# First feed-forward product of a two-layer trunk: four of seven half products joint in 512 columns, one weight sum loaded anew, weight splits handed out one unit later

## The chip, the cores and the metric

One core of one Trainium2 chip. The metric is the device time of one execution in microseconds, lower is better. The engines meant below are PE (TensorE, matrix products), DVE (VectorE), ACT (ScalarE), POOL (GpSimd) and SP (SyncE, which here only issues DMAs). PE writes its sums to PSUM; everything else lies in SBUF.

## The reference

A sequence of 512 positions with 1024 features passes two layers. Each has an attention part and then a dense part with 4096 hidden features; the change touches the dense part alone:

```
y = rmsnorm(x, g_ff)
x = x + (square(relu(y @ W1))) @ W2      # W1: 1024 x 4096, W2: 4096 x 1024, float32
```

The kernel keeps nearly float32 accuracy with PE's faster fp32r type: a value is split into a rounded part (hi) and the rest (lo), and a product is three matmuls, hi by hi, hi by lo and lo by hi, summed in PSUM.

## The kernel before

**Two products, each in seven parts.** The hidden features are handled in four groups (`g`) per layer. In a group both products, `h @ W1` and then `F @ W2`, are done with seven block products instead of eight (Strassen's scheme in Winograd's form): sums and differences of quarter blocks are made first, seven half-size products follow, and the results are added up. The first product has the halves "1" to "7" (`HALVES`, L50), each for `c` = 0 and 1, so 14 units per group; the kernel calls these units q. A q unit is 24 matmuls of 128 weights by 256 moving columns: eight weight blocks, and for each the three products of `three` (L295 to L300). The second product has seven forms ("11", "21", "x1" and so on) of two f units each, with 48 matmuls of 512 columns per form.

**Weights.** `_Weights` holds one list of units. A unit's raw weights come by DMA as 512 KB. `split_part` makes the pair: ACT copies raw to fp32r, `whi` (L131), DVE subtracts to get `wlo` (L132). The feed-forward part has five such pairs. `next` (called when a unit's matmuls are written) calls `do_split`, which writes the split of the unit four ahead and then what hangs on that unit in `then`: a weight sum (`sum1`, L859, on DVE in L862), a load (`fetch`, L869, and `fill`, L850, on SP), or a load that the DMA adds to what is in SBUF (issued by POOL in L852, L864, L876). The sum for half "7" is made in that last way in `sum1` (L864): the raw block of half "1" stays in its buffer and POOL adds another block to it.

**Moving operands.** `h_hi` and `h_lo` are the split of the normalised x; `T_hi` and `T_lo` that of its differences, which `opening(0)` to `opening(3)` make (L884: one DVE operation, then ACT for hi and DVE for lo in L245) during the first group of a layer. `MOVES` says which half reads which 256 columns of h or T.

**Taps.** When a unit's matmuls are written, `tap` (L960) writes what empties its PSUM bank: ACT copies (L970, L975, L977), DVE adds (L972, L978, L983). `bend` queues relu and square on ACT (L967) in `put_off`, and `come_to` writes the queued work behind the next unit's split. The results are F[0] to F[3]; for F[3] (half "4") relu reads PSUM directly. `behind_3` makes the differences of F for the second product (F4 in L1001, F0 in L1003, F1 in L996), and `roll` splits F[1] and F[3] into `Ah` and `Al`, the moving operand of forms "11" and "21" (forms "x1" to "x4" read splits of the other F, `Ahx` and `Alx`). `gather` adds the sums of the forms into Y (L1025).

**Order.** ACT and DVE run in the order in which the program writes their work: `line` chains them. An instruction whose input is not there holds up all behind it on its engine. PE's order is the program's too, with a few matmuls pulled ahead by the scheduler. The loads are `paced` by the last split.

Of the kernel before, what the change touches and what calls it, by code (L numbers as in the profile page):

```python
# [17 lines left out]
P = 128  # L18
# [31 lines left out]
HALVES = ("1", "2", "5", "6", "7", "3", "4")  # L50
LAYS = (("5", 1), ("6", 0), ("6", 1), ("7", 0))
# [46 lines left out]
class _Weights:  # L98
    def __init__(self, nc, dram, rawp, splp):
        self.nc, self.dram, self.rawp = nc, dram, rawp  # L100
        self.loaded = self.split = self.used = self.turn = 0
        self.raw, self.tiles, self.home, self.then, self.lows, self.came = {}, {}, {}, {}, {}, {}
# [44 lines left out]
    def do_split(self, n, ahead=None):  # L147
        while self.split < min(n, self.stop):
            i = self.split
            kind = _UNITS[i][0]  # L150
            if ahead is not None and i > ahead and self.owner.get(self.spot(i), -1) >= ahead:
                break
            if kind not in "fq":
                self.load(_SLOT[i] + 1)
            self.split_part(i, 0, 1024)
# [21 lines left out]
def trunk(ctx, tc, xT, w, w1, w2, gains, gfin, lamv, cos, sin, out):  # L177
# [8 lines left out]
    banks = {"t": 2, "mm": 2, "s": 3, "o": 1}  # L186
    turn = [0]

    def bank(tag, name):
        if tag == "any":  # L190
            tag = ("mm", "s", "s", "mm", "s")[turn[0] % 5]
            turn[0] += 1
        return ps.tile([P, 512], F32, tag=tag, name=name, bufs=banks[tag])
# [6 lines left out]
    h_hi = cp.tile([P, KC, S], F32R, tag="h_hi", name="h_hi")  # L200
    h_lo = cp.tile([P, KC, S], F32R, tag="h_lo", name="h_lo")
# [132 lines left out]
    for l in range(L):  # L334
        last = l == L - 1
        with ExitStack() as actx:
# [496 lines left out]
            T_hi = fr.tile([P, KC, S], F32R, tag="T_hi", name=f"T_hi{l}")  # L833
            T_lo = fr.tile([P, KC, S], F32R, tag="T_lo", name=f"T_lo{l}")
# [11 lines left out]
            def fill(what, g, c):  # L846
                t = homes[(what, c)] if what in "yw" else kept["x.z".index(what)][c]
                for q in {"y": "1", "z": "2", "x": "5", "w": "4"}[what] + {"y": "7", "x": "63"}.get(what, ""):
                    W.raw[_AT[("q", l, g, q, c)]] = t
                paced(nc.sync.dma_start(t, quad1(g, {"y": "11", "z": "12", "x": "21", "w": "22"}[what], c)))  # L850
                if what == "x":
                    nc.gpsimd.dma_start(t, quad1(g, "22", c), accum_op=ALU.add)  # L852
# [6 lines left out]
            def sum1(what, g, c):  # L859
                i = _AT[("q", l, g, "5", c)]  # L860
                t, by = W.raw[i], W.raw[_AT[("q", l, g, "1" if what == "y" else "2", c)]]
                line(v=nc.vector.tensor_add(t, t, by))  # L862
                if what == "y":
                    nc.gpsimd.dma_start(by, quad1(g, "21", c), accum_op=ALU.add)  # L864
# [14 lines left out]
            def then(kind, g, form, c, fn, *args):  # L879
                W.then.setdefault(_AT[(kind, l, g, form, c)], []).append(lambda: fn(*args))  # L880

# [24 lines left out]
            for g in range(GROUPS):  # L906
                for c in range(GP // 2):
                    then("q", g, "5", c, sum1, "y", g, c)
                    then("q", g, "6" if g else "7", c, sum1, "z", g, c)
                    then("q", g, "2" if g else "7", c, fetch, g, "21", c)  # L910
# [23 lines left out]
        with ExitStack() as fctx:  # L934
# [7 lines left out]
            for c in range(GP // 2):  # L942
                fill("w", 0, c)
            W.free = False
            MOVES = {"1": (0, hi_t, 0), "2": (4, hi_t, 0), "3": (4, lo_t, 0), "4": (4, hi_t, 1), "5": (0, hi_t, 1),
                     "6": (4, lo_t, 1), "7": (0, lo_t, 1)}

            def mover(q, cc):
                k, t, which = MOVES[q]
                a, b = ((h_hi, h_lo), (T_hi, T_lo))[which]  # L950
                return a[:, k + cc, t], b[:, k + cc, t]
# [8 lines left out]
            def tap(q, c, pt):  # L960
                def f(n):
                    return F[n][:, 512 * c : 512 * c + 512]

                def bend(n, scale=1.0, src=None):
                    for o, i, fn, by in ((f(n), src, AF.Relu, scale), (f(n), None, AF.Square, 1.0)):
                        put_off.append(lambda o=o, i=i, fn=fn, by=by: line(
                            nc.scalar.activation(o, o if i is None else i, fn, scale=by)))  # L967

                if q == "1":
                    line(nc.scalar.copy(f(1), pt))  # L970
                elif q == "2":
                    line(v=nc.vector.tensor_add(f(1), f(1), pt))  # L972
                    bend(1)
                elif q == "6":
                    line(nc.scalar.copy(f(0), pt))  # L975
                elif q == "7":
                    line(nc.scalar.copy(f(2), pt))  # L977
                    line(v=nc.vector.tensor_add(f(2), f(2), sums[("b", c)]))  # L978
                    bend(2, -1.0)
                elif q == "4":  # L980
                    bend(3, -1.0, pt)
                elif q == "3":
                    line(v=nc.vector.tensor_add(f(0), f(0), pt))  # L983
                    bend(0)
# [3 lines left out]
            def roll(form):  # L988
                nm = f"{form}{l}"
                hi = rolls.tile([P, 1024], F32R, tag="Ah", name="Ah" + nm)  # L990
                lo = rolls.tile([P, 1024], F32R, tag="Al", name="Al" + nm)
                rolled[form] = hi, lo
                return split(hi, lo, F[FSLOT[form]])
# [13 lines left out]
            def behind_4(late=False):  # L1007
                line(*roll("21"))
                if late:
                    less(1, 4, 1)  # L1010
                less(3, 1, 3)
# [18 lines left out]
            def turned(tb, j):  # L1030
                pt = bank("t", f"xT{tb}{j}")
# [19 lines left out]
            def back(c):  # L1051
                pt = bank("t", f"yT{l}{c}")
# [54 lines left out]
            for g in range(GROUPS):  # L1107
                end = g == GROUPS - 1
                kinds = iter(("s", "s", "s", "mm", "mm", "o"))
                for q in HALVES:  # L1110
                    for c in range(GP // 2):
                        n = {("2", 0): 1, ("5", 0): 2, ("3", 0): 3}.get((q, c))
# [4 lines left out]
                        spot = {"1": "a", "2": "c", "5": "b", "3": "b"}.get(q, "a")  # L1117
                        if q in "125":
                            sums[(spot, c)] = bank(next(kinds), f"f{q}{l}{g}{c}")
                        pt = sums[(spot, c)]  # L1120
                        for i in range(2):
                            for cc in range(4):
                                ops = three(pt[:, 256 * i : 256 * i + 256], wpair(u, 4 * i + cc), mover(q, cc),
                                            q in "125" and i == cc == 0, i == 1 and cc == 3, q not in "125")
                                if i == cc == 0 and (q, c) != ("1", 0):
                                    behind(ops[0], pe_end)
                        pe_end = ops[2]
                        tap(q, c, pt)
                        if (g, q, c) == (1, "1", 0):
                            ptr = bank("t", f"rs_m{l}")  # L1130
# [14 lines left out]
                        if g == 0 and (q, c) == ("4", 0):  # L1145
                            put_off.append(lambda: behind_3(1))
                        if c:
                            put_off.append({
                                "27"[g == 0]: lambda: line(*roll("11")),
                                "3": lambda: behind_3(0 if g == 0 else None),  # L1150
                                "4": lambda: behind_4(g == 0),
                            }.get(q, lambda: None))
                come_to()
                chains = {}
                for f, form in enumerate(FORMS):
                    chain, i, j = TAPS[form]
                    fresh_bank = chain not in chains
                    if fresh_bank:
                        chains[chain] = [bank(("s", "s", "s", "mm", "mm", "o")[2 * len(chains) + r], f"{form}{l}{g}{r}")
                                         for r in range(2)]  # L1160
# [4 lines left out]
                    for r in range(2):  # L1165
# [38 lines left out]
                        if end and not last:  # L1204
# [4 lines left out]
                            if form == "x4":  # L1209
                                for c_ in CAME[2 * r : 2 * r + 2]:  # L1210
                                    back(c_)
# [104 lines left out]
```

## Time and profile before

| | us |
|---|---|
| median of three runs | 1120.8 (1119.42 to 1121.47) |
| the profiled execution | 1119.62 |
| its span in the profile | 1117.8 |
| PE busy | 1109.3 |
| DVE busy | 929.5 |
| ACT busy | 709.5 |
| the q units of group 0, layer 0 | 239.96 to 280.27 |
| the q units of group 2, layer 0 | 398.33 to 438.64 |

The span leaves out 1.82 us that lie around it in the profiled execution. Times inside it are given in us from the span's start. The page of the profile lists busy time by engine, then groups of equal instructions; the timeline lists single instructions with the idle time ahead of each and what ended it; a view of windows sums a stretch by engine. A matmul's duration there includes its passage through the array and overlaps the next one, so PE's rate is read from the distance of starts.

### The profile page before, as it was taken

What the parts mean: (1) busy time and instruction counts of PE and PEld (TensorE: products, weight loads), DVE (VectorE), ACT (ScalarE), POOL (GpSimd) and SP (SyncE); (2) the same over time, 40 slices, a digit from 0 to 9 for tenths busy, and PEclk for the clock granted to TensorE, in tenths of its full rate; (3) what the DMA queues carried; (4) which work ended last, traced back from release to release, by engine and by line L of the source; (5) the groups of instructions that cost most, each with busy time, mean ns of one, the idle gap of its engine ahead of it and who ended that gap; (6) DMA issues with size and microseconds to landing.
All of it is one profiled execution on the core that took longest, in us unless ns stands there. A gap on an engine that the chain in (4) does not pass through costs nothing.

```text
span 1117.8 us, 17696 instructions
## 1 busy us (share of the span) xinstructions
PE 1109.3 (99%) x6654; PEld 985.1 (88%) x6654; DVE 929.5 (83%) x1230; ACT 709.5 (63%) x1113; POOL 176.9 (16%) x257
## 2 busy tenths in 40 slices
PE   9999999999999999999999999999999999999997
PEld 7888989889889899899888889888998998998986
DVE  7878789788897877878888787897988888888787
ACT  6546666677767557567555467675777665565675
POOL 1001334210210110201000014440101102011022
PEclk9999999999999999999999999999999999999999
DMA  7746334266887776876537463523578768859665
GB/s 249 208 123 203 114 116 114 81 170 188 186 197 214 167 176 204 189 190 158 123 113 208 119 177 113 157 77 142 105 229 185 189 189 187 206 138 202 172 135 148
DMA packets 60613, 183.37 MB, mean 164 GB/s; under 512 B 7536, under 2 KB 8816, under 8 KB 60528
## 3 DMA queue, kind: packets, MB, share of 16 engines
q1 hardware_dynamic: 46416, 131.62, 37.1%
q0 software_dynamic: 13824, 50.34, 25.7%
q8 instruction: 53, 0.87, 0.3%
q10 hardware_dynamic: 288, 0.28, 0.1%
q14 instruction: 32, 0.26, 0.1%
HBM read 154.95 MB, written 2.10 MB: 140 GB/s over the span
## 4 chain that ended last, share of the span: by engine, by line
PE 85%; DVE 5%; DMA 4%; issue 3%; ACT 2%; POOL 1%; POOLq 0%; DVEq 0%; SPq 0%; ACTq 0%
PE f L300 8%; PE f L298 8%; PE f L299 8%; DMA q<-in_w 3%; PE x L299 2%; PE x L298 2%; PE x L300 2%; PE wo L298 2%; PE wo L299 2%; PE wo L300 2%; DVE wlo L132 1%; DMA st1d1q<-hl1d1k 1%; PE T1s L623 1%; PE T0s L623 1%; PE v0u L298 1%
## 5 line engine op out<-in xcount | busy, mean ns | idle before, releaser
L132 DVE TENSOR_TENSOR wlo<-q,whi 128x1024 fp32r<-128x1024 f32 x184 | 223.6, 1220 | 23.9 <-ACT whi L131 22.6
L131 ACT ACTIVATE whi<-q 128x1024 fp32r<-128x1024 f32 x184 | 191.2, 1052 | 65.3 <-DMA q<-in_w 32.3
L298 PE MATMUL f<-T_hi,whi 128*128 128x256 f32 x512 | 145.5, 284 | 0.0
L300 PE MATMUL f<-T_hi,wlo 128*128 128x256 f32 x512 | 144.9, 283 | 0.0
L299 PE MATMUL f<-T_lo,whi 128*128 128x256 f32 x512 | 144.9, 283 | 0.0
L876 POOL DMA_DIRECT2D q<-in_w x64 | 56.2, 913 | 366.2 <-DVE wlo L132 346.4
L298 PE MATMUL f<-h_hi,whi 128*128 128x256 f32 x384 | 108.8, 283 | 0.0
L299 PE MATMUL f<-h_lo,whi 128*128 128x256 f32 x384 | 108.7, 283 | 0.0
L300 PE MATMUL f<-h_hi,wlo 128*128 128x256 f32 x384 | 108.7, 283 | 0.0
L299 PEld LDWEIGHTS f<-T_lo,whi 128*128 128x128 f32 x512 | 98.3, 192 | 0.0
L298 PEld LDWEIGHTS f<-T_hi,whi 128*128 128x128 f32 x512 | 98.3, 192 | 0.0
L300 PEld LDWEIGHTS f<-T_hi,wlo 128*128 128x128 f32 x512 | 98.2, 192 | 0.0
L967 ACT ACTIVATE F<-F 128x512 f32<-128x512 f32 x112 | 70.4, 629 | 21.7 <-DVE F L972 17.8
L131 ACT ACTIVATE whi<-raw 128x1024 fp32r<-128x1024 f32 (+1 forms) x58 | 55.7, 970 | 31.7 <-PE wo L299 6.9
L298 PEld LDWEIGHTS f<-h_hi,whi 128*128 128x128 f32 x384 | 73.7, 192 | 0.4
L299 PEld LDWEIGHTS f<-h_lo,whi 128*128 128x128 f32 x384 | 73.7, 192 | 0.3
L300 PEld LDWEIGHTS f<-h_hi,wlo 128*128 128x128 f32 x384 | 73.7, 192 | 0.1
L132 DVE TENSOR_TENSOR wlo<-raw,whi 128x1024 fp32r<-128x1024 f32 (+1 forms) x58 | 68.1, 1186 | 5.7 <-ACT whi L131 5.7
L245 ACT ACTIVATE Ahx<-F 128x1024 fp32r<-128x1024 f32 x32 | 34.0, 1061 | 52.1 <-PE x L299 24.4
L245 DVE TENSOR_TENSOR Alx<-F,Ahx 128x1024 fp32r<-128x1024 f32 x32 | 39.2, 1225 | 8.6 <-ACT Ahx L245 8.6
L245 DVE TENSOR_TENSOR Al<-F,Ah 128x1024 fp32r<-128x1024 f32 x24 | 29.4, 1224 | 18.0 <-ACT Ah L245 18.0
L556 POOL TENSOR_TENSOR sig1s<-sig1s,C1s 128x128 f32<-128x128 f32 (+3 forms) x32 | 28.5, 892 | 57.6 <-DVE C1s L553 46.7
(994 smaller groups left out, 3242.0 us busy)
## 6 DMA issues: line engine op xcount, KB each, us to landing
q<-in_w SPq DMA_DIRECT2D x100, 512.0 KB, 5.1
q<-in_w POOLq DMA_DIRECT2D x84, 512.0 KB, 7.0
raw<-in_w SPq DMA_DIRECT2D x62, 512.0 KB, 4.2
yw<-in_w SPq DMA_DIRECT2D x12, 512.0 KB, 4.5
yw<-in_w POOLq DMA_DIRECT2D x12, 512.0 KB, 5.6
cs<-in_w SPq DMA_DIRECT2D x8, 512.0 KB, 7.9
ww<-in_w SPq DMA_DIRECT2D x8, 512.0 KB, 4.0
x<-in_xT SPq DMA_DIRECT2D x8, 256.0 KB, 4.2
```

The costliest lines, as they stand in the source:

```text
L131: h = nc.scalar.activation(hi[:, a:b], raw[:, a:b], AF.Copy)
L132: self.last = h, nc.vector.tensor_tensor(out=lo[:, a:b], in0=raw[:, a:b], in1=hi[:, a:b].bitcast(F32), op=ALU.subtract)
L245: return nc.scalar.activation(hi, src, AF.Copy), nc.vector.tensor_tensor(out=lo, in0=src, in1=hi.bitcast(F32), op=ALU.subtract)
L298: return (nc.tensor.matmul(pt, ah, bh, start=first, stop=False, skip_group_check=onto), nc.tensor.matmul(pt, ah, bl, start=False, stop=Fal ...
L299: nc.tensor.matmul(pt, ah, bl, start=False, stop=False, skip_group_check=onto),
L300: nc.tensor.matmul(pt, al, bh, start=False, stop=last, skip_group_check=onto))
L556: nc.gpsimd.tensor_mul(sig[:, 0:wd], sig[:, 0:wd], C[:, 1 : wd + 1])
L623: nc.tensor.transpose(pt[:, n * P : (n + 1) * P], u["w"][qi][:, kb * P : (kb + 1) * P], ident)
L876: paced(nc.gpsimd.dma_start(t, quad(g, q, c), accum_op=ALU.add))
L967: nc.scalar.activation(o, o if i is None else i, fn, scale=by)))
```

## The change

- **Order of halves**: "1", "2", "6", "5", "3", "7", "4" in place of "1", "2", "5", "6", "7", "3", "4".
- **Joint halves**: for "1", "2", "6" and "4", `whi` by hi and `whi` by lo become one matmul of 512 columns (two runs of 256, h_hi and h_lo now being halves of one tile, as T_hi and T_lo are). It leaves hi and lo sums side by side in a full bank, two banks per unit in place of one. `wlo` by hi stays a matmul of 256 columns. A unit is then 16 matmuls and not 24; "5", "3" and "7" stay as they were.
- **Taps**: the two sides have to be added when they are read. "1" is copied by ACT from PSUM to PSUM (two of 512); "2", "7" and "4" read in pieces of 256, by ACT and by DVE; "6" goes to F[0] and to a bank `fb` in four ACT copies of 256; "3" and "5" accumulate on `fb`. For F[3] the order is now ACT copies, DVE adds, ACT relu and square. F[3] is rolled in two halves of 512, the first behind unit 4 c0.
- **Weights**: half "7" loads its first block again (SP) and POOL adds the other, rather than building on the buffer of half "1": 16 more loads of 512 KB. The sum for "6" is written just ahead of its split (`first`).
- **Splits**: `W.next("q", 1)` hands out a split one unit later, three ahead of the one whose matmuls are written.

In all ACT gets 120 more instructions, DVE 72, SP 16 more loads, and PE 1024 matmuls of 256 columns become 512 of 512.

```diff
-HALVES = ("1", "2", "5", "6", "7", "3", "4")
+HALVES = ("1", "2", "6", "5", "3", "7", "4")
...
-                for q in {"y": "1", "z": "2", "x": "5", "w": "4"}[what] + {"y": "7", "x": "63"}.get(what, ""):
+                if what == "7":
+                    t = homes["y", c] if g else (F[3], kept[1][0])[c]
...
-                if what == "x":
-                    nc.gpsimd.dma_start(t, quad1(g, "22", c), accum_op=ALU.add)
+                if what in "x7":
+                    nc.gpsimd.dma_start(t, quad1(g, "22" if what == "x" else "21", c), accum_op=ALU.add)
...
-                if what == "y":
-                    nc.gpsimd.dma_start(by, quad1(g, "21", c), accum_op=ALU.add)
...
+                def take(n, kind, lows):
+                    for h, t in zip(halves, sums[kind, c]):
+                        line(nc.scalar.copy(F[n][:, h], t[:, 256:512] if lows else t[:, 0:256]))
+
+                def more(n, kind, lows):
+                    for h, t in zip(halves, sums[kind, c]):
+                        line(v=nc.vector.tensor_add(F[n][:, h], F[n][:, h], t[:, 256:512] if lows else t[:, 0:256]))
...
                 elif q == "4":
-                    bend(3, -1.0, pt)
+                    take(3, "a", True)
+                    more(3, "a", False)
+                    bend(3, -1.0)
...
-                        u = W.next("q")
+                        u = W.next("q", 1)
...
+                                if joint:
+                                    steps[0].append((both_of(to), a[0], moved[2]))
+                                    steps[1].append((to[:, 0:256], a[1], moved[0]))
...
-                        if g == 0 and (q, c) == ("4", 0):
-                            put_off.append(lambda: behind_3(1))
+                        if (q, c) == ("4", 0):
+                            put_off.append(lambda: line(*roll("21", 0, 512)))
+                            if g == 0:
+                                put_off.append(lambda: behind_3(1))
```

**DVE where the q units of group 2, layer 0, end and form "21" begins.** The names: `F30` is F[3], `F40`, `F00`, `F10` the results that `behind_3` makes, `wlo104` and `wlo105` the two units of form "21", `Al210` the lo part of the rolled F[3]; the numbers behind an underscore only tell tiles apart. Before, from the last add into F[0] to the first gathering into Y:

```order
L983 TENSOR_TENSOR F00_2566<-F00_2566,f5021_4436 128x512
L132 TENSOR_TENSOR wlo104_4650<-q10_0_2560,whi104_4649 128x1024
L1001 TENSOR_TENSOR F40_2757<-F20_2568,F00_2566 128x1024
L1003 TENSOR_TENSOR F00_2566<-F10_2567,F00_2566 128x1024
L996 SCALAR_TENSOR_TENSOR F10_2567<-F40_2757,F10_2567 128x1024
L132 TENSOR_TENSOR wlo105_4684<-q11_0_2561,whi105_4683 128x1024
L245 TENSOR_TENSOR Al210_4717<-F30_2569,Ah210_4716 128x1024
L996 SCALAR_TENSOR_TENSOR F30_2569<-F10_2567,F30_2569 128x1024
L1025 TENSOR_TENSOR Y0_2756<-Y0_2756,11020_4721 128x512
L1025 TENSOR_TENSOR Y0_2756<-Y0_2756,11021_4722 128x512
L245 TENSOR_TENSOR Alx10_4764<-F40_2757,Ahx10_4763 128x1024
```

Of the change, from the row behind F4 (`F40`) on:

```order
L1043 TENSOR_TENSOR F00_2564<-F10_2565,F00_2564 128x1024
L1036 SCALAR_TENSOR_TENSOR F10_2565<-F40_2755,F10_2565 128x1024
L997 TENSOR_TENSOR F30_2567<-F30_2567,fa0200_4197 128x256
L997 TENSOR_TENSOR F30_2567<-F30_2567,fa0201_4198 128x256
L132 TENSOR_TENSOR wlo104_4583<-q10_0_2559,whi104_4582 128x1024
L254 TENSOR_TENSOR Al210_4590<-F30_2567,Ah210_4589 128x512
L997 TENSOR_TENSOR F30_2567<-F30_2567,fa0210_4199 128x256
L997 TENSOR_TENSOR F30_2567<-F30_2567,fa0211_4200 128x256
L254 TENSOR_TENSOR Al210_4590<-F30_2567,Ah210_4589 128x512
L1036 SCALAR_TENSOR_TENSOR F30_2567<-F10_2565,F30_2567 128x1024
L1065 TENSOR_TENSOR Y0_2754<-Y0_2754,11020_4618 128x512
L132 TENSOR_TENSOR wlo105_4646<-q11_0_2560,whi105_4645 128x1024
```

The split of `wlo105` has moved from the place behind `F10`, ahead of the roll, to a place behind four adds, both halves of the roll and a row of Y. On ACT `whi105` moved alike: it stood ahead of relu and square of F[3], and now stands behind them and both rolled halves:

```order
L993 COPY F30_2567<-fa0200_4197 128x256
L993 COPY F30_2567<-fa0201_4198 128x256
L131 ACTIVATE whi104_4582<-q10_0_2559 128x1024
L989 ACTIVATE F30_2567<-F30_2567 128x512 x2
L254 ACTIVATE Ah210_4589<-F30_2567 128x512
L993 COPY F30_2567<-fa0210_4199 128x256
L993 COPY F30_2567<-fa0211_4200 128x256
L989 ACTIVATE F30_2567<-F30_2567 128x512 x2
L254 ACTIVATE Ah210_4589<-F30_2567 128x512
L131 ACTIVATE whi105_4645<-q11_0_2560 128x1024
L254 ACTIVATE Ahx10_4665<-F40_2755 128x1024
```

Each `x2` is a relu and a square. ACT's copies from `fa` come first, and between them and these two DVE must have added.

**PE at the start of form "21", group 2, layer 0.** The rows with the waits that they carry. Before, from the first matmul of the form:

```order
L298 MATMUL 21020_4749<-whi104_4649,Ah210_4716 128x512 [waits PE_49,Activation_49]
L299 MATMUL 21020_4749<-wlo104_4650,Ah210_4716 128x512 [waits DVE_49]
L300 MATMUL 21020_4749<-whi104_4649,Al210_4717 128x512 [waits DVE_49]
L298 MATMUL 21020_4749<-whi104_4649,Ah210_4716 128x512
L299 MATMUL 21020_4749<-wlo104_4650,Ah210_4716 128x512
L300 MATMUL 21020_4749<-whi104_4649,Al210_4717 128x512
L298 MATMUL 21020_4749<-whi105_4683,Ah210_4716 128x512
L299 MATMUL 21020_4749<-wlo105_4684,Ah210_4716 128x512
```

Of the change, from the seventh:

```order
L307 MATMUL 21021_4652<-whi104_4582,Ah210_4589 128x512 [waits PE_49]
L307 MATMUL 21020_4651<-whi105_4645,Ah210_4589 128x512 [waits Activation_49]
L308 MATMUL 21021_4652<-wlo104_4583,Ah210_4589 128x512
L309 MATMUL 21021_4652<-whi104_4582,Al210_4590 128x512
L307 MATMUL 21021_4652<-whi104_4582,Ah210_4589 128x512
L308 MATMUL 21021_4652<-wlo104_4583,Ah210_4589 128x512
L309 MATMUL 21021_4652<-whi104_4582,Al210_4590 128x512
L307 MATMUL 21021_4652<-whi105_4645,Ah210_4589 128x512
L307 MATMUL x1020_4695<-whi106_4669,Ahx10_4665 128x512 [waits PE_49,Activation_49]
L307 MATMUL x1021_4696<-whi106_4669,Ahx10_4665 128x512 [waits PE_49]
L308 MATMUL 21020_4651<-wlo105_4646,Ah210_4589 128x512 [waits DVE_49]
```

Of the first product of the form, the second unit's weights (`whi105`) are wanted by the seventh matmul before and by the eighth in the change. What follows in the change is mixed with matmuls of form "x1", whose operands `Ahx10` and `whi106` ACT makes behind `whi105`.

**ACT and PE in the first group of layer 0.** ACT in the change from the tap of unit 1 c0 (the bank `fa` copied to the bank `fc`) on; `T0` is T_hi by `opening(1)`, `whi36` the weights of unit 6 c0:

```order
L1002 COPY fc0000_2783<-fa0000_2763 128x512
L1002 COPY fc0001_2784<-fa0001_2764 128x512
L254 ACTIVATE T0_2563<-hx0mdl_2569 128x4x256
L131 ACTIVATE whi36_2791<-q10_0_2559 128x1024
L1002 COPY fc0010_2811<-fa0010_2765 128x512
L1002 COPY fc0011_2812<-fa0011_2766 128x512
L131 ACTIVATE whi37_2816<-q11_0_2560 128x1024
L993 COPY F10_2565<-fc0000_2783 128x256
```

PE before, where unit 2 c0 ends (`f2000`) and 2 c1 begins (`f2001`):

```order
L298 MATMUL f2000_2834<-h_hi_73,whi34_2673 128x256
L299 MATMUL f2000_2834<-h_lo_74,whi34_2673 128x256
L300 MATMUL f2000_2834<-h_hi_73,wlo34_2674 128x256
L298 MATMUL f2001_2866<-h_hi_73,whi35_2711 128x256
L299 MATMUL f2001_2866<-h_lo_74,whi35_2711 128x256
```

PE in the change at the same place (`fc0001` and `fc0010`):

```order
L1174 MATMUL fc0001_2784<-h_73,wlo34_2672 128x256
L1174 MATMUL fc0001_2784<-h_73,whi34_2671 128x512
L1174 MATMUL fc0001_2784<-h_73,wlo34_2672 128x256
L1174 MATMUL fa0001_2764<-T0_2563,whi36_2791 128x512 [waits Activation_49]
L1174 MATMUL fc0010_2811<-h_73,whi35_2709 128x512 [waits Activation_49]
L1174 MATMUL fc0010_2811<-h_73,wlo35_2710 128x256
```

A matmul of unit 6 c0 stands ahead of unit 2 c1 here and waits for `whi36`, and the first of 2 c1 waits for the copy that ACT makes behind it. Before, 2 c1 followed 2 c0 with nothing of a later unit between them.

More of the change, by code (lines that the diff above doesn't have):

```diff
@@ L154, in do_split @@
                 self.load(_SLOT[i] + 1)
+            self.first.pop(i, lambda: None)()
             self.split_part(i, 0, 1024)
@@ L184, in trunk, with one, some @@
     ps = ctx.enter_context(tc.tile_pool(name="ps", bufs=2, space=PSUM))
-    banks = {"t": 2, "mm": 2, "s": 3, "o": 1}
+    banks = {"t": (0, 1), "mm": (2, 3), "s": (4, 5, 6), "o": (7,)}
+    calls = dict.fromkeys(banks, 0)
+    def one(k, name):
+        return ps.tile([P, 512], F32, tag=f"k{k}", name=name, bufs=1)
+    def some(ks, name):
+        return [one(k, f"{name}{n}") for n, k in enumerate(ks)]
     turn = [0]
@@ L949, in mover @@
                 k, t, which = MOVES[q]
-                a, b = ((h_hi, h_lo), (T_hi, T_lo))[which]
-                return a[:, k + cc, t], b[:, k + cc, t]
+                m = (h2, T2)[which]
+                return m[:, 0, k + cc, t], m[:, 1, k + cc, t], m[:, :, k + cc, t]
             sums, put_off = {}, []
@@ L969, in tap @@
                 if q == "1":
-                    line(nc.scalar.copy(f(1), pt))
+                    sums["c", c] = some((4 + 2 * c, 5 + 2 * c), f"fc{l}{g}{c}")
+                    for to, t in zip(sums["c", c], sums["a", c]):
+                        line(nc.scalar.copy(to, t))
                 elif q == "2":
-                    line(v=nc.vector.tensor_add(f(1), f(1), pt))
-                    bend(1)
-                elif q == "6":
-                    line(nc.scalar.copy(f(0), pt))
+                    take(1, "c", False)
@@ new lines, in tap @@
+                    more(1, "c", True)
+                elif q == "6":
+                    take(0, "a", False)
+                    sums["b", c] = one(4 + c, f"fb{l}{g}{c}")
+                    for i, t in enumerate(sums["a", c]):
+                        line(nc.scalar.copy(sums["b", c][:, 256 * i : 256 * i + 256], t[:, 256:512]))
+                    bend(1)
+                elif q == "5":
+                    line(nc.scalar.copy(F[2][:, at : at + 512], sums["b", c]))
+                elif q == "3":
+                    o = F[0][:, at : at + 512]
+                    line(v=nc.vector.tensor_add(o, o, sums["b", c]))
+                    bend(0)
@@ L986, in trunk, with roll @@
+                    bend(3, -1.0)
             rolled = {}
[L988 to L993, printed above, removed]
+            def roll(form, a=0, b=1024):
+                if a == 0:
+                    nm = f"{form}{l}"
+                    rolled[form] = [rolls.tile([P, 1024], F32R, tag=t, name=t + nm) for t in ("Ah", "Al")]
+                hi, lo = rolled[form]
+                return split(hi[:, a:b], lo[:, a:b], F[FSLOT[form]][:, a:b])
@@ L1030, in turned @@
             def turned(tb, j):
-                pt = bank("t", f"xT{tb}{j}")
+                pt = one(6 + (tb + j) % 2, f"xT{tb}{j}")
                 for k in range(4):
@@ L1116, in trunk @@
                         come_to()
[L1117 to L1120, printed above, removed]
+                        spot = {"2": "c", "5": "b", "3": "b"}.get(q, "a")
+                        if (q, c) == ("1", 0):
+                            for c_ in range(GP // 2):
+                                sums["a", c_] = some((2 * c_, 2 * c_ + 1), f"fa{l}{g}{c_}")
@@ L1121, in trunk @@
+                        pt = sums[spot, c]
                         for i in range(2):
+                            joint, onto = q in "1264", q != "1"
+                            to = pt[:, 256 * i : 256 * i + 256] if spot == "b" else pt[i] if joint else pt[i][:, 0:256]
+                            steps = [[] for _ in range(2)]
                             for cc in range(4):
-                                ops = three(pt[:, 256 * i : 256 * i + 256], wpair(u, 4 * i + cc), mover(q, cc),
-                                            q in "125" and i == cc == 0, i == 1 and cc == 3, q not in "125")
@@ new lines, in trunk @@
+                            steps = steps[0] + steps[1] if q == "4" or not joint else [s_ for p_ in zip(*steps) for s_ in p_]
+                            for n_, s_ in enumerate(steps):
+                                op = nc.tensor.matmul(*s_, start=q == "1" and n_ == 0, stop=n_ == len(steps) - 1,
+                                                      skip_group_check=onto)
+                                if i == n_ == 0 and (q, c) != ("1", 0):
+                                    behind(op, pe_end)
@@ L1158, in trunk @@
                     if fresh_bank:
-                        chains[chain] = [bank(("s", "s", "s", "mm", "mm", "o")[2 * len(chains) + r], f"{form}{l}{g}{r}")
-                                         for r in range(2)]
+                        k = (6, 4, 0)[len(chains)]
+                        chains[chain] = some((k, k + 1), f"{form}{l}{g}")
                     to = chains[chain]
```

91 lines of the change are left out of this document (50 added, 41 removed).

## The prediction

> **What bounds the kernel now.** I read the page first (busy time by engine, clock), then PE's waits, then windows of the feed-forward stages, then single rows of the timeline.
>
> ```profile
> PE 1109.3 (99%) x6654; PEld 985.1 (88%) x6654; DVE 929.5 (83%) x1230; ACT 709.5 (63%) x1113; POOL 176.9 (16%) x257
> PEclk9999999999999999999999999999999999999999
> ...
> PE warm L231 <- POOL edge L225: 1.4, 1, 1.4
> PE wo L298 <- ACT vdh L245: 0.2, 1, 0.2
> PE 11001_3231 L298 <- DVE Y L1025: 0.2, 1, 0.2
> ...
> 240.00:252.00 12.00, 12.00 (x102) 12.00 (x101) 10.81 (x12) 8.39 (x11) 1.76 (x2) 1.00 0.57 88
> 398.00:436.00 38.00, 38.00 (x317) 37.92 (x316) 29.14 (x28) 24.70 (x34) 3.73 (x5) 1.00 0.72 189
> 436.00:474.00 38.00, 38.00 (x180) 31.94 (x179) 32.82 (x34) 22.37 (x24) 6.02 (x7) 1.00 0.81 187
> ```
>
> The window rows give the stretch, then busy time of PE, PEld, DVE, ACT and POOL, then clock and DMA. PE is busy 99% of the span at full clock, waits 1.8 us in all, and in the feed-forward windows it never stops. So PE's own work is the bound, and DVE is near behind: 10.81 of 12 us in group 0, 32.82 of 38 around the end of a q phase. Anything that puts DVE or ACT ahead of PE turns into time.
>
> **The gain on PE.** Rates from distances of starts:
>
> ```profile
> 239.96 0.28 PE L298 MATMUL f<-h_hi,whi 128*128 128x256 f32 x1
> 280.27 0.40 PE L298 MATMUL 11000_3230<-whi,Ah 128*128 128x512 f32 x1
> ...
> 386.77 0.39 PE L298 MATMUL 11011_3988<-whi,Ahx 128*128 128x512 f32 x1
> 398.33 0.28 PE L298 MATMUL f<-h_hi,whi 128*128 128x256 f32 x1
> ```
>
> Between the first two lie 14 units of 24 matmuls of 256 columns: 40.31 / 336 = 0.1200 us each. Between the others lie 51 of 512: 11.56 / 51 = 0.2267. One joint matmul replaces two: 0.2399 - 0.2267 = 0.0133 us. There are 8 per unit, 8 joint units per group, 8 groups: 512 x 0.0133 = **6.8 us less**. A joint unit takes 8 x (0.2267 + 0.1200) = 2.77 us, a plain one 2.88.
>
> The Trainium skill, "TensorE: Matmul & The Clock Gate", section "Wait — 56ns, not 53.3ns?", gives a warm matmul N/2.4 ns plus about 2.5 ns fixed; a merged pair would then save only 2.5 ns, 1.3 us in all. The rows speak against it: their fixed part is 0.2399 - 0.2267, 13 ns, and the sum goes by them.
>
> **What the taps cost.** Rows of one q phase and the end of it:
>
> ```profile
> L131 ACT ACTIVATE whi<-q 128x1024 fp32r<-128x1024 f32 x22 | 22.9, 1054 | 11.7 <-DMA q<-in_w 3.3 <-PE f L300 3.1 <-PE 11011_3988 L300 2.2
> L967 ACT ACTIVATE F<-F 128x512 f32<-128x512 f32 x14 | 8.8, 629 | 2.9 <-DVE F L972 2.6
> L970 ACT COPY F<-f 128x512 f32<-128x512 f32 x2 | 1.1, 568 | 0.0
> L972 DVE TENSOR_TENSOR F<-F,f 128x512 f32<-128x512 f32 x2 | 1.4, 678 | 0.0
> ```
>
> 256 wide copies and adds aren't in the trace. Drawn on from 512 and 1024 they are 0.36 (ACT: 0.57 less half of 1.05 - 0.57, so 0.33 to 0.36) and 0.42 us (DVE: 0.68 less half of 1.22 - 0.68); a lower end is half a 512 (0.28, 0.34), an upper end a whole one (0.57, 0.68). I take the drawn ones, being nearest in shape. The 120 extra ACT instructions are 15 a group, some 5 us beside 24.70 of 38; DVE's 72 are 9 a group, some 3.5 beside 29.14 (net of the adds and copies of 512 that go). In the middle of a q phase of groups 1 to 3 both fit beside PE and I cost them at nothing; without that cover it would be up to those 5 us a group. ACT's copy from PSUM to PSUM isn't in the trace either; I take it as 0.57, and between 0.28 and 1.1 it stays under a unit's 2.77 us.
>
> **What the loads cost.** Sixteen more loads and as many adding ones as before, by:
>
> ```profile
> q<-in_w SPq DMA_DIRECT2D x100, 512.0 KB, 5.1
> q<-in_w POOLq DMA_DIRECT2D x84, 512.0 KB, 7.0
> ```
>
> The pair for "7" goes out behind the split of "6" (SP past the other loads, POOL behind it), about 5.5 us into the phase, and lands 12.1 later at 17.6; its split is wanted at about 20. Nothing, with 2 us of cover; if the cover is gone, up to 3 us a group. Dropping POOL's wait for half "1" frees nothing that PE waits for.
>
> **The end of the q phase** is where the cost lies. Before:
>
> ```profile
> 433.08 0.69 DVE L983 TENSOR_TENSOR F<-F,f 128x512 f32<-128x512 f32 x1 [0.68 <-PE f L300]
> 434.06 1.23 DVE L132 TENSOR_TENSOR wlo<-q,whi 128x1024 fp32r<-128x1024 f32 x1 [0.28 <-DMA ww<-in_w]
> 435.24 1.23 DVE L1001 TENSOR_TENSOR F<-F,F 128x1024 f32<-128x1024 f32 x1
> 436.50 1.23 DVE L1003 TENSOR_TENSOR F<-F,F 128x1024 f32<-128x1024 f32 x1
> 437.76 1.23 DVE L996 SCALAR_TENSOR_TENSOR F<-F,F 128x1024 f32<-128x1024 f32 x1
> 438.90 1.22 DVE L132 TENSOR_TENSOR wlo<-q,whi 128x1024 fp32r<-128x1024 f32 x1
> 441.23 1.23 DVE L245 TENSOR_TENSOR Al<-F,Ah 128x1024 fp32r<-128x1024 f32 x1 [1.11 <-ACT Ah L245]
> ...
> 439.47 0.64 ACT L967 ACTIVATE F<-F 128x512 f32<-128x512 f32 x1
> 440.14 1.06 ACT L245 ACTIVATE Ah<-F 128x1024 fp32r<-128x1024 f32 x1
> ...
> 438.64 0.40 PE L298 MATMUL 11020_4721<-whi,Ah 128*128 128x512 f32 x1
> 444.11 0.39 PE L298 MATMUL 21020_4749<-whi,Ah 128*128 128x512 f32 x1
> ```
>
> All that form "21" needs was there at 442.46, 1.65 us ahead of its start. Now the same stage of the change, in the order of rows shown above, from E, the start of unit 4 c0. DVE adds into F[2] until 1.0, ACT bends it until 2.3, DVE makes F4, F0 and F1 until 6.0 (3.66, as from 435.24 to 438.90). Only then can it add F[3] c0 (6.8); ACT bends (8.1), rolls half (0.63, to 8.75), and only behind that copies c1 (9.4); DVE adds (10.2), ACT bends (11.5), rolls (12.2), and splits `whi105` (13.3). PE reaches form "21" at 5.54 + 5.47 = 11.0 and wants `whi105` seven matmuls later, at 12.6: it waits 0.75. Behind `whi105` ACT makes Ahx and `whi106` (15.3), wanted at 14.95: 0.4. DVE: Al, the last difference and a row of Y, then `wlo105` at 16.0, wanted at 15.8: 0.25; then Y, Alx and `wlo106` at 19.0, wanted at 18.3: 0.7. Sum **2.1 us**. The order is the same in groups 1 to 3 of both layers: 6 x 2.1 = **12.6 us**. With every step 0.08 shorter (DVE's rows start 0.08 before the last ends: 438.90 after 437.76 + 1.23) it is about 0.6 a group, with 256 wide pieces at their upper ends about 3. The split handed out late is half of the reason, the adds behind the three differences the other half.
>
> **Group 0** has the differences of h and x besides. Before:
>
> ```profile
> 242.65 1.22 DVE L862 TENSOR_TENSOR q<-q,q 128x1024 f32<-128x1024 f32 x1
> 243.80 1.28 DVE L245 TENSOR_TENSOR h_lo<-hx0mdl,h_hi 128x512 fp32r<-128x512 f32 x2
> 247.39 1.22 DVE L890 SCALAR_TENSOR_TENSOR hx0mdl<-hx0mdl,hx0mdh 128x1024 f32<-128x1024 f32 x1
> ...
> 242.16 1.14 ACT L245 ACTIVATE h_hi<-hx0mdl 128x512 fp32r<-128x512 f32 x2
> ```
>
> In the change the sums stand behind `opening(1)`, so its operation starts when h_lo is done, near 244.0. Then, each waiting for the one ahead: T_hi 246.4, T_lo 247.6, the sum 248.8, `whi36` 249.9, ACT's copy into the bank of 2 c1 250.5. PE stands at 239.96 + 3 x 2.77 = 248.3: **2.2 us**. From 250.5 PE does 2 c1, 6 and 5 until 264.6. ACT empties 6 c0 in four pieces (257.4) and splits for unit 3 (258.4), DVE makes the lo (259.7) and `opening(2)` (260.9), ACT T_hi (262.0), a split (263.0), bends (264.3) and then the copy out of `fb` that unit 3 c0 waits for (264.9): 0.4 with its hand-over. After 3 and 7 PE is at 276.5. There a pulled-ahead matmul of form "11" wants weights that ACT splits behind `opening(3)` (DVE 272.9 after the add into F[0], T_hi 274.0), a split (275.0), bends (276.2) and Ah (277.2): 278.2, **1.7**. Form "21", chained as above, starts at 289.2; its `whi` for the second unit is wanted at 291.7 and there at 292.8, that of form "x1" wanted at 293.3 and there at 294.9: **2.7**. Together 7.0, two layers **14.0 us**; between 2.2 (the first alone) and 9 (each full, with the first not giving the later ones time).
>
> **Sum** against the profiled execution, 1119.62 (span 1117.8 and 1.82 around it; the median of the runs, 1120.8, is 1.2 above): 1119.6 - 6.8 + 12.6 + 14.0 = **1139.4 us**.
>
> **Rivals.**
> 1. *The slack holds, the result is faster.* Its mechanism is at the end of the q phase: DVE and ACT run each step as soon as its input is there, and overlaps of 0.1 in some twenty steps take off the 2.1. It decides when the waits fall under 6.8 in all, under 0.85 a group. For it: 1.65 us of slack before, and PE's waits before were 0.2 at most here. Against it: the chain passes between ACT and DVE five times, where before ACT bent F[3] straight from PSUM, behind no add of DVE's. Without waits: 1119.6 - 6.8 = 1112.8; with 0.85 a group 1119.6.
> 2. *Half the waits.* The pulled-ahead matmul of group 0 costs its 2.2, the rest half: 1119.6 - 6.8 + 6.3 + 7 = 1126.
> 3. *PE doesn't gain as said.* Two runs of 256 columns, or sums side by side, cost what two matmuls do: no 6.8, so 1146. By the page's fixed part it would be 1145. For it: PEld is busy 37.92 of 38 in the q phase, so loads of weights may set the rate; but joint halves need a third fewer.
>
> **How the numbers follow.** Forecast as summed (1130 to 1148 with its own bounds): 0.40. Half: 0.22. No gain on PE: 0.10. Slack holds: 0.28, of it 0.23 faster and 0.05 within 0.2% (about what a measurement of this kernel can tell from no change). With 0.02 of the half case also within it: faster 0.23, same 0.07, slower 0.70. The range has to take in the slack case, 1112 to 1148.
>
> **What would show it.** Right: starts of joint units 2.77 apart; PE's waits list, 1.8 us before, near 25, with `whi` and `wlo` ahead of form "21" and `whi36` ahead of 2 c1 in group 0; DVE's difference rows back to back ahead of the adds in 256. Wrong: PE unbroken at form "21" (the chain is shorter than I walked it), joint units of 2.88 (rival 3), or a wait for the load of "7" (its cover fails).

## The result, and the profile after

The change makes the kernel slower: **1171.47 us** (median of 4 runs, 1169.48 to 1173.49) against 1120.56 us for the kernel before on the same chip; the ratio is 1.0455, interval 1.0432 to 1.0478. The forecast was slower by 19 us; it is slower by 51. Of the two runs of experiment e2 below, one went at a granted clock of 0.654 from end to end (1561 us) and is left out, so e2's figure is a single run.

The chain that ended last (the waits and the work followed back from the last instruction), on the page of the profile before; then, of the change, span, busy time by engine and the same chain:

```profile
PE 85%; DVE 5%; DMA 4%; issue 3%; ACT 2%; POOL 1%; POOLq 0%; DVEq 0%; SPq 0%; ACTq 0%
...
span 1168.4 us, 16918 instructions
...
PE 1125.7 (96%) x6142; PEld 959.4 (82%) x6142; DVE 936.2 (80%) x1302; ACT 745.0 (64%) x1249; POOL 177.9 (15%) x257
...
PE 46%; DVE 16%; DMA 15%; issue 12%; ACT 10%; POOL 1%; SPq 0%; POOLq 0%; DVEq 0%; ACTq 0%
DMA q<-in_w 9%; DMA yw<-in_w 5%; DVE wlo L132 5%; ACT whi L131 4%; ACT F L989 2%; DVE q L873 2%; DVE F L997 1%; PE x L308 1%; PE x L307 1%; PE x L309 1%; PE wo L307 1%; PE wo L308 1%; PE wo L309 1%; DVE yw L873 1%; PE fb L1174 1%
```

Before, the chain was 85% PE; now it is 46%, and loads of weights carry 15%: `yw` is the buffer of the reloaded sum. DVE is busy for 7 us more than before and ACT for 36 (it ran 136 more instructions, 1249 for 1113, not 120), in a span that is 51 us longer. PE's waits after (what it waited for, us in total, times, longest), and one row of ACT's:

```profile
PE fa L1174 <- DVE F L997: 10.7, 5, 2.8
PE x L307 <- ACT whi L131: 4.2, 5, 1.6
PE fa L1174 <- ACT whi L131: 4.0, 2, 2.5
PE 21120_10183 L307 <- ACT whi L131: 1.9, 1, 1.9
...
ACT whi L131 <- DMA yw<-in_w: 31.6, 6, 6.4
```

The first row was in no step of the prediction: before unit 4 c0 may add to its bank `fa`, DVE must have read the sums of half 7 there. The last row names the source: six times, for up to 6.4 us, ACT stands on the load of `yw`. The chain inside group 2 of layer 0 (whose first unit starts at 412.73), in order of time, start and duration:

```profile
424.37 1.23 DVE wlo L132
425.59 1.15 DVE q L873
426.74 0.02 SPq L862
426.76 0.03 issue
426.79 6.64 DMA yw<-in_w
433.43 0.40 issue
433.82 8.75 DMA yw<-in_w
442.58 0.02 issue
442.60 1.07 ACT whi L131
443.67 0.02 issue
443.69 1.24 DVE wlo L132
```

The buffer of 7 c1 is that of 6 c1. The split of 6 c1 and the sum for half 3 behind it (`q`, L873), which reads the same buffer, end at 426.7; only then does SP load the block for 7 c1, and only when that has landed does POOL add the other. ACT has its weights at 442.6, 29.9 us into the phase. The timelines of ACT, DVE and PE there:

```profile
435.64 0.59 ACT L1013 COPY F<-fb 128x512 f32<-128x512 f32 x1 [0.19 <-PE fb L1174]
442.60 1.06 ACT L131 ACTIVATE whi<-yw 128x1024 fp32r<-128x1024 f32 x1 [6.37 <-DMA yw<-in_w]
...
443.69 1.22 DVE L132 TENSOR_TENSOR wlo<-yw,whi 128x1024 fp32r<-128x1024 f32 x1 [6.98 <-ACT whi L131]
...
450.10 0.75 DVE L997 TENSOR_TENSOR F<-F,fa 128x256 f32<-128x256 f32 x2
...
450.66 1.62 PE L1174 MATMUL fa<-T,whi 128*128 128x512 f32 x3 [2.79 <-DVE F L997]
```

Both engines stand some 7 us, though PE still has units to do. All that is queued behind the split comes late: the roll, relu and square, the adds of halves 3 and 7, until unit 4 c0 waits 2.79 us for the add at 450.10.

Lengths of the phases of the first product (q) and of what follows each up to the next (f), summed over the groups named. They are worked out from the starts on PE's timelines: a phase begins with its first matmul (single ones pulled ahead into the phase before are not counted), and the last f ends with the last matmul. An f phase is seven forms of 24 matmuls (168 in the trace, not 48 a form); that of layer 0's last group also takes in the attention part of layer 1. The columns after the first are differences from it:

| us | before | change | e5 | e8 | e10 | e12 |
|---|---|---|---|---|---|---|
| q, groups 0 | 80.6 | +12.6 | +12.3 | +12.4 | +11.6 | +10.0 |
| f, groups 0 | 78.6 | +2.3 | +4.2 | +2.5 | +2.4 | +1.0 |
| q, groups 1 to 3 | 245.7 | +13.2 | -2.8 | -2.8 | -2.8 | +8.2 |
| f, groups 1 to 3 | 466.1 | +23.2 | +13.0 | +23.4 | +8.3 | +9.5 |
| sum | | +51.2 | +26.7 | +35.5 | +19.5 | +28.7 |

### The profile page after: what moved, and what is told of

The parts are those of the page before. It is cut to its first block, busy times and chain, and to the rows that moved or that the text cites. A ratio compares the mean times of both kernels' runs of the same rounds, so it can differ in the third digit from the quotient of the medians.

```text
span 1168.4 us, 16918 instructions
## 1 busy us (share of the span) xinstructions
PE 1125.7 (96%) x6142; PEld 959.4 (82%) x6142; DVE 936.2 (80%) x1302; ACT 745.0 (64%) x1249; POOL 177.9 (15%) x257
## 4 chain that ended last, share of the span: by engine, by line
PE 46%; DVE 16%; DMA 15%; issue 12%; ACT 10%; POOL 1%; SPq 0%; POOLq 0%; DVEq 0%; ACTq 0%
DMA q<-in_w 9%; DMA yw<-in_w 5%; DVE wlo L132 5%; ACT whi L131 4%; ACT F L989 2%; DVE q L873 2%; DVE F L997 1%; PE x L308 1%; PE x L307 1%; PE x L309 1%; PE wo L307 1%; PE wo L308 1%; PE wo L309 1%; DVE yw L873 1%; PE fb L1174 1%
## 5 line engine op out<-in xcount | busy, mean ns | idle before, releaser
L1174 PE MATMUL fa<-T,whi 128*128 128x512 f32 (+1 forms) x512 | 130.3, 346 | 14.8 <-DVE F L997 10.7
L1174 PEld LDWEIGHTS fa<-T,whi 128*128 128x128 f32 x512 | 87.2, 193 | 25.8 <-ACT F L989 11.6
L1174 PE MATMUL fa<-T,wlo 128*128 128x256 f32 x384 | 93.2, 285 | 0.7 <-DVE wlo L132 0.7
L132 DVE TENSOR_TENSOR wlo<-yw,whi 128x1024 fp32r<-128x1024 f32 x36 | 44.0, 1223 | 58.6 <-ACT whi L131 58.6
L1174 PEld LDWEIGHTS fa<-T,wlo 128*128 128x128 f32 x384 | 69.3, 193 | 4.2 <-DVE wlo L132 1.1
L254 DVE TENSOR_TENSOR Al<-F,Ah 128x1024 fp32r<-128x1024 f32 (+1 forms) x32 | 30.5, 954 | 24.8 <-ACT Ah L254 24.8
L1174 PE MATMUL fc<-h,whi 128*128 128x512 f32 x128 | 48.8, 419 | 0.0
L1174 PE MATMUL fb<-h,whi 128*128 128x256 f32 x256 | 47.0, 285 | 0.8 <-ACT F L1013 0.8
L1174 PE MATMUL fb<-T,whi 128*128 128x256 f32 x256 | 46.5, 283 | 0.0
L1174 PE MATMUL fa<-h,whi 128*128 128x512 f32 x128 | 45.6, 398 | 0.0
L1174 PEld LDWEIGHTS fb<-h,whi 128*128 128x128 f32 x256 | 39.8, 192 | 1.2 <-ACT F L1013 1.2
```

What stands on the lines that cost most here:

```text
L132: self.last = h, nc.vector.tensor_tensor(out=lo[:, a:b], in0=raw[:, a:b], in1=hi[:, a:b].bitcast(F32), op=ALU.subtract)
L254: return nc.scalar.activation(hi, src, AF.Copy), nc.vector.tensor_tensor(out=lo, in0=src, in1=hi.bitcast(F32), op=ALU.subtract)
L1174: op = nc.tensor.matmul(*s_, start=q == "1" and n_ == 0, stop=n_ == len(steps) - 1, skip_group_check=onto)
```

## The experiments

Each ran beside the kernel before on one chip. Times are medians; ratios are to the kernel before as measured beside it, and the intervals in brackets are 95%.

**e1, half 7 subtracted.** The weights of 7 are those of 6 less those of 4, made in place by DVE; no load.

```diff
+            def lower(g, c):
+                t, by = (W.raw[_AT[("q", l, g, q, c)]] for q in "74")
+                line(v=nc.vector.tensor_sub(t, t, by))
...
+                    first("q", g, "7", c, lower, g, c)
```

> The weights of half 7 are made by DVE from those of 6 and 4 (7 = 6 - 4, in place) instead of a new load and an adding load. Theory A (the reloaded sum lands late, ACT stands on it for up to 6.4 us in each of groups 1 to 3, and the waits ahead of unit 4 c0 and a part of those at form 21 follow from it): ACT's wait for yw goes from 31.6 us to near 0, PE's waits for DVE's adds ahead of 4 c0 (10.7 us) nearly vanish, the time falls by 20 to 28 us to 1143 to 1151. Theory B (DVE and ACT are simply overfull in the q phase): DVE has 2.4 us more per group, the waits ahead of 4 c0 stay, 1165 to 1185.

1161.04 us, 1.0365 (1.0335 to 1.0395): a miss between both theories. ACT's wait for the load of `yw` and PE's wait for DVE's adds ahead of 4 c0 are gone from the lists, as A has it. What came in their place:

```profile
PE 11000_3189 L307 <- ACT whi L131: 3.6, 1, 3.6
PE 11100_8664 L307 <- ACT whi L131: 3.6, 1, 3.6
...
ACT whi L131 <- DVE yw L874: 17.6, 12, 2.6
```

L874 is the subtraction: ACT now waits 17.6 us for it. In group 0, where DVE is fullest, the weights of form "11" come 3.6 us late instead of 1.3. One wait was exchanged for another, so this run can't price the load.

**e2, the adding load left out.**

```diff
-                if what in "x7":
+                if what == "x":
```

> The adding load of half 7 is left out (its weights lack one block), the new load stays. Theory A: the sum lands with SP's load, some 9 us sooner, ACT's wait for it goes to about 0 to 1 us, time 1143 to 1153, like the run with the subtraction less its DVE work. Theory B: no change within 5 us of 1171.

1149.37 us, in A's range; it is a single run, and no more is drawn from it.

**e3, splits one unit earlier**, in the change as it is: `W.next("q")` for `W.next("q", 1)`.

> Only the splits of the first product are handed out one unit earlier again, as before the change. Theory A: the split that stands on the late load now stands one unit earlier in ACT's queue and holds up more; what form 21 gains (up to 12 us) is given back, 1165 to 1185. Theory C (the prediction's: the splits handed out late are the main loss): 1155 to 1161.

1173.90 us, 1.0480 (1.0447 to 1.0512): A holds, C falls. ACT waits as long for the load, and PE meets it earlier: at `fb`, in unit 3 c1 (in group 2 of layer 0), and not ahead of 4 c0:

```profile
PE fb L1174 <- ACT F L1013: 14.0, 6, 3.0
PE fc L1174 <- ACT fc L1002: 9.9, 14, 2.0
...
ACT whi L131 <- DMA yw<-in_w: 31.8, 6, 6.0
```

**e4, e1 and e3 together.**

> Both: half 7 subtracted and splits one unit earlier. Theory A and C together: the waits at form 21 for whi of its second unit go too, 8 to 14 us below the run with the subtraction alone, 1131 to 1142. Theory A alone: no better than the subtraction alone, within 4 us of it.

1157.49 us, 1.0333 (1.0303 to 1.0364), 3.6 below e1: not the gain that A and C together ask for, and within what A alone allows. The waits for `whi` at form "21" are gone, and PE waits 11.3 us for `fc`, the copy of half 1's sums, in their place.

**e5, the reloaded sum loaded early.** Only its buffer and its moment change.

```diff
-                    t = homes["y", c] if g else (F[3], kept[1][0])[c]
+                    t = (F[3], F[4] if g else kept[1][0])[c]
...
-                        then("q", g, "6", c, fill, "7", g, c)
+                        then("q", g, "2", c, fill, "7", g, c)
```

> Only the place and the moment of the reloaded sum are changed: in groups 1 to 3 it goes into F[3] and F[4], which are free then, and is issued behind the splits of half 2 (at the start of the phase), not behind those of half 6. The bytes, DVE's and ACT's work are as in the change. Theory A (the load is late because its buffer comes free late): ACT's wait for the sum of 7 (31.6 us) goes, the waits ahead of 4 c0 in groups 1 to 3 (11 us of PE and the slow clock behind them) go, 1145 to 1153. Theory B (ACT and DVE are overfull anyway): 1162 to 1173.

**1146.68 us**, 1.0231 (1.0216 to 1.0246), 24.8 below the change: A is shown. The bytes and the work are the same; only the load's buffer, and with it the moment at which it may start, is different. The window of the q phase of group 2, layer 0, of the change and then of e5 (length, then busy PE, PEld, DVE, ACT, POOL, then clock and DMA):

```profile
412.73:457.67 44.94, 41.65 (x273) 38.12 (x272) 30.07 (x33) 27.92 (x46) 4.36 (x5) 0.96 0.68 183
...
408.40:448.30 39.90, 39.90 (x273) 36.90 (x273) 30.59 (x33) 28.06 (x46) 4.20 (x5) 1.00 0.80 217
```

DVE and ACT are as busy (30.1 and 30.6, 27.9 and 28.1), and PE never stops in e5. So the taps' extra work does fit beside PE in groups 1 to 3, as the prediction said; the load did not. Of the 24.8 us some 3.4 are two stretches of half clock that came with the waits (see the last section).

**e6, e5 with each joint matmul split in two.**

```diff
-                                    steps[0].append((both_of(to), a[0], moved[2]))
+                                    steps[0].append([(to[:, 256 * e : 256 * e + 256], a[0], moved[e]) for e in range(2)])
```

> On top of the early load each joint matmul is two of 256 columns again, into the same two halves of the bank; taps, order and splits stay joint. Theory D (a joint matmul followed by one of 256 columns takes 0.236 + 0.117 us in the trace where 0.240 + 0.120 did before, so it saves 6.7 ns, not 13.3): 3 to 4 us above the run with the early load. The prediction's rate: 6.8 above it. If PE's waits take up the difference: within 1 us.

1149.92 us, 1.0263 (1.0246 to 1.0280), 3.2 above e5, with intervals that touch. The traces say it more firmly. The first matmul of the q phase of group 3, layer 0, and the first behind it, in e5 and then in e6:

```profile
488.97 0.39 PE L1174 MATMUL fa<-h,whi 128*128 128x512 f32 x1
528.81 0.40 PE L307 MATMUL 11030_5324<-whi,Ah 128*128 128x512 f32 x1
...
488.09 0.40 PE L1178 MATMUL fa<-h,whi 128*128 128x256 f32 x2
528.40 0.40 PE L307 MATMUL 11030_5580<-whi,Ah 128*128 128x512 f32 x1
```

39.84 us against 40.31, both without a stop: 0.47 a group, 3.8 for eight, 0.47 / 64 = 7.3 ns for each joint matmul. D holds: in this mix, each joint one followed by one of 256 columns, half of the rate that was read from 512 behind 512 is left.

**e7, e5 with nothing pulled ahead.** The first matmul of either bank of a unit is chained behind the last of the one before.

```diff
-                                if i == n_ == 0 and (q, c) != ("1", 0):
+                                if n_ == 0 and (i, q, c) != (0, "1", 0):
                                     behind(op, pe_end)
-                        pe_end = op
+                            pe_end = op
```

> On top of the early load no matmul of a later unit may stand ahead of a unit's last (the matmul of unit 6 c0 that PE does ahead of 2 c1 in group 0 goes back). Theory E (ACT's order is what holds: the copy for 2 c1 stands behind the same split in ACT's queue): within 2 us of the run with the early load. Theory F (the pulled-ahead matmul is the cause of the 2.6 and 1.7 us there): 4 to 7 us faster.

1148.16 us, 1.0243 (1.0228 to 1.0259): E holds, F falls. The wait keeps its place and changes its name, in e5 and then in e7:

```profile
PE fa L1174 <- ACT whi L131: 3.7, 2, 2.1
...
PE fc L1174 <- ACT fc L1002: 4.9, 2, 2.9
```

**e8, e5 with the differences behind the adds into F[3].**

```diff
-                                "7": lambda: behind_3(0 if g == 0 else None),
+                                "7": lambda: behind_3(0) if g == 0 else None,
...
                 line(*roll("21", 512, 1024))
+                if not late:
+                    behind_3()
```

> On top of the early load the three differences F4, F0, F1 of groups 1 to 3 are written behind DVE's adds into F[3] and not ahead of them. Theory G (these adds, queued behind 3.7 us of differences, are what makes form 21 late): the waits for whi at form 21 go, those for wlo and for form x1 stay in part, 4 to 10 us faster than the early load alone. Theory H (the split one unit later is all of it): within 3 us.

1155.57 us, 1.0308 (1.0292 to 1.0323), 9 slower than e5: neither range is met, and the gain that G asks for is not there. `whi105` is on time, but `wlo105` now stands behind four whole passes of DVE, and PE waits for it in all six groups, as here:

```profile
PE 21020_4651 L308 <- DVE wlo L132: 2.1, 1, 2.1
```

Most of the 9 us is not these waits themselves. Beside five of the six, the granted clock stands at 0.50 for 3.41 us, which costs about 1.7 us each, 8.5 in all; e5 has no such stretch in groups 1 to 3.

**e9, e5 with `opening(1)` one unit later**: `("2", 0): 1` for `("1", 1): 1`.

> On top of the early load, opening(1) is written one unit later, ahead of unit 2 c0: on ACT T_hi now stands behind the copies for 2 c1, on DVE its operation behind the first sum. Theory E (ACT's order is what holds up 2 c1 in group 0): the 2.2 and 1.8 us ahead of 2 c1 go in both layers, 3 to 6 us faster than the early load alone. If DVE is the limit there, the wait moves to unit 6 c0: within 1.5 us of it.

1145.07 us, 1.0224 (1.0205 to 1.0243), 1.6 below e5, and not told apart from it: not the gain that E asks for. The wait ahead of 2 c1 is gone, and is met again at unit 3 c0, behind `opening(2)`, a place that neither case had named:

```profile
PE fb L1174 <- ACT F L1013: 4.7, 2, 2.4
```

ACT's order decided where PE stood; the wait in group 0 doesn't go by moving one step.

**e10, e5 with the last split on time.**

```diff
-                        u = W.next("q", 1)
+                        u = W.next("q", int((q, c) != ("4", 1)))
```

> On top of the early load only the very last split of each q phase (second unit of form 21) is handed out one unit earlier, at unit 4 c1, ahead of relu and square of F[3]; all others stay one later. Theory H (this split, pushed behind the F[3] chain, is what makes form 21 wait, 2.2 us a group): 5 to 12 us faster than the early load alone. Theory I (DVE's and ACT's work in that stretch is too much in whatever order): within 3 us.

**1140.14 us**, 1.0181 (1.0166 to 1.0196); against e5's 1.0231 that is 0.50% or 5.6 us, at the low end of H. The f phases of groups 1 to 3 keep +8.3 of +13.0, so the split pushed behind the F[3] chain is about a third of what they had. At the place itself it is more: in the first 15.5 us of these phases, where forms "21" and "x1" lie, PE's starts come 9.4 us late in e5 and 3.8 in e10 (the sum of what distances of starts have beyond 0.2267 us, over the six groups). What PE still waits for there, in group 0 as well, is DVE:

```profile
PE x L308 <- DVE wlo L132: 4.3, 8, 1.2
```

**e11, e9 and e10 together.**

> Early load, opening(1) later and the last split on time together: if E and H hold, both gains add up, 9 to 17 us below the early load alone, 1130 to 1138; still above the kernel before, as groups 0 keep their other waits and joint halves give 3 to 4 us only.

1139.33 us, 1.0170 (1.0150 to 1.0191), the lowest median here, above the expected range and not told apart from e10. The gains don't add up.

**e12, e5 with all splits earlier.**

> On top of the early load all splits of the first product are handed out one unit earlier, as before the change. If handing out later only costs (theory H for all splits), 1138 to 1141 or below, as with the last split alone on time. If it also pays, since ACT's copy of half 1's sums then stands behind one split more and unit 2 waits for it (as PE's waits for fc, 11.3 us, in the run with both the subtraction and earlier splits), the gain at form 21 is given back at 2 c0: 1142 to 1152.

1147.96 us, 1.0237 (1.0194 to 1.0279): not told apart from e5. The f phases of groups 1 to 3 gain 3.5 us (+9.5 for +13.0) and group 0 5.5, and the q phases of groups 1 to 3 lose 11.0 (from -2.8 to +8.2), for the reason expected:

```profile
PE fc L1174 <- ACT fc L1002: 10.4, 14, 2.3
```

Handing out one unit later is thus no loss on the whole: it has ACT's copy of half 1's sums ready in time, and costs at form "21". The kernel before stays the fastest; the nearest version is 1.7% slower.

## Why the prediction was wrong

The direction was right, and most of the mechanisms that it named are in the traces; the time lay 32 us above the forecast of 1139.4.

1. **The step that failed** is the price of the loads: "goes out behind the split of '6' ..., about 5.5 us into the phase, and lands 12.1 later at 17.6 ... Nothing, with 2 us of cover". In the change SP issues them at 9.4 and 14.1 us into the phase (422.11 and 426.79 after 412.73). I counted from where the split of 6 is written; the buffer comes free only when that split, and the sum for half 3 that reads it too, have run. The first pair landed at 20.2, just in time, the second at 29.9. Of the second, SP's part took 6.64 and POOL's 8.75 us, both above the medians of 5.1 and 7.0, with six more loads issued between 428 and 438. The price without cover, "up to 3 us a group", was too small as well: e5 puts the late load at 24.8 us, 4.1 for each of the six groups. One late buffer stops ACT, ACT's order stops DVE, and the backlog meets PE twice, ahead of unit 4 and at form "21" (+23.2 against +13.0 in the table). The prediction named a wait for this load as a sign that it would be wrong, and gave it no case and no chance.
2. **The gain on PE** was about half: 3.8 us for 6.8. The rate of 512 columns came from a row of such matmuls one behind the other; the change sets one of 256 behind each, and a joint unit takes 2.82 us, not 2.77. Rival 3 (no gain) fell: e6 loses 0.47 us a group. The Trainium skill, "TensorE: Matmul & The Clock Gate", section "Wait — 56ns, not 53.3ns?", gives about 2.5 ns fixed for each warm matmul, by which a merged pair saves 2.5 ns (an estimate from that figure); it is not borne out either, since e6 and e5 differ by 7.3 ns for each joint matmul.
3. **Form "21"**: 2.1 us a group and 12.6 in all were forecast. With the load out of the way (e5) the f phases of groups 1 to 3 are 13.0 longer, but that the sizes meet is partly luck. At forms "21" and "x1", where the four waits were forecast, PE's starts come 9.4 us late (1.5 to 1.9 a group); the rest lies later, where nothing was forecast. The wait for `whi105`, 0.75 in the forecast, shows as 0.2 or not at all. The two reasons were put at half each: with the last split on time (e10) 5.5 of the 9.4 go, a little more than half; that the adds behind the differences are the rest is not shown, since moving them (e8) makes `wlo105` late in their place.
4. **Group 0**: 14.0 us of waits less 1.7 of gain, 12.3, were forecast; e5 shows 16.5 (12.3 in the q phases and 4.2 in the f phases), the change 14.9. The first wait was 2.5 and 1.6 us (2.2 forecast), the second 0.4 in both layers (0.4), the third 1.3 in both (1.7). The first is followed in both layers by 3.41 us at a clock of 0.50, 1.7 us each, which was in no sum. The pulled-ahead matmul, to which the first wait was laid beside ACT's copy, has no part in it (e7).
5. **Taps at nothing** in groups 1 to 3 held: e5's q phases there run without a stop. The pieces cost what was drawn on: in the change ACT's copies of 256 took 0.37 us (0.36), DVE's adds 0.41 (0.42), ACT's copy from PSUM to PSUM 0.57 (0.57). DVE's "some 3.5" us more a group was too high even by these prices (twelve adds of 256 and two of 512 for six of 512 are 2.3). Rivals 1 and 2 (slack that holds, half the waits) fell; rival 2's own terms, with the 2.2 in full, come to 1128 and not 1126.

Left open: what in group 0 would have to move for its waits to go. e7 and e9 only show that single moves shift them.

## What to carry to other kernels

A reload into a buffer still in use starts when the buffer's last reader has run, not where the program writes the load. Work out its landing from that instant, with the slower end of the landings that the profile lists. An engine that runs in program order and meets the load late is to be charged with all that is queued behind it. And take a matmul's rate from rows of the mix that the change will run, not from rows of one shape.

## What the runs showed of the hardware

A wait can be followed by more lost time than its length. Windows of the change around four waits of PE (unit 2 c0 to 2 c1 in group 0, then unit 4 c0 in groups 1, 2 and 3 of layer 0; length, busy times, then the granted clock):

```profile
251.00:256.00 5.00, 4.96 (x18) 4.03 (x19) 3.86 (x4) 3.54 (x7) 0.00 (x0) 0.66 0.01 3
364.00:369.00 5.00, 4.41 (x16) 3.77 (x17) 4.51 (x8) 4.49 (x8) 1.10 (x2) 0.66 0.31 84
450.00:453.00 3.00, 2.34 (x7) 1.98 (x8) 2.73 (x6) 2.97 (x5) 0.28 (x1) 0.53 0.00 0
536.00:540.00 4.00, 3.58 (x20) 3.15 (x21) 3.51 (x6) 3.94 (x6) 0.88 (x1) 1.00 0.60 188
```

At three of them the mean clock is 0.53 to 0.66: inside the window it stands at 0.50 for 3.41 us, from 252.18, 364.82 and 450.15 on. At the last, with a wait as long (2.79 us, like the third), it stays at 1.00. In layer 1 a wait of 1.56 us came with such a stretch (from 832.45), and in e10 one of 1.9 (`fb`, group 0) with none. So the length of the wait alone does not decide it, and what does is not shown. What it looks like on PE:

```profile
252.86 0.41 PE L1174 MATMUL fc<-h,wlo 128*128 128x256 f32 x1
253.07 0.63 PE L1174 MATMUL fc<-h,whi 128*128 128x512 f32 x1
253.50 0.41 PE L1174 MATMUL fc<-h,wlo 128*128 128x256 f32 x1
```

From 252.86 to 253.50 a pair takes 0.64 us; at full clock in group 2 sixteen pairs take 5.64 (412.73 to 418.37), 0.35 each. The change has four such stretches up to its last matmul, e5 two, e8 seven, e10 none.

A row of the list of waits is also shorter than the time that PE loses by it. In e5 at form "21" and behind it:

```profile
458.23 0.50 PE L308 MATMUL 21020_4651<-wlo,Ah 128*128 128x512 f32 x1
...
460.44 0.40 PE L309 MATMUL 21021_4652<-whi,Al 128*128 128x512 f32 x1
461.10 0.50 PE L308 MATMUL x<-wlo,Ahx 128*128 128x512 f32 x1 [0.27 <-DVE wlo L132]
461.44 0.40 PE L309 MATMUL x<-whi,Alx 128*128 128x512 f32 x1
```

The wait is listed with 0.27 us. From 460.44 to 461.10 are 0.66, 0.44 more than the usual 0.2267, and the next start comes 0.11 late as well. In this f phase the listed idle time is 0.8 us, and the phase is 2.6 longer than before. The forecast counted a wait at its length and had no term for the clock.
